# The opening of a hybrid layer: forget-gate columns behind the value weights, and their column chunk multiplied last

## The chip, the core and the metric

The kernel runs on one core of one Trainium2 chip. The metric is the device time of one execution in microseconds. The core has a matrix engine (TensorE, PE in the profile), three engines that work on tiles in SBUF and PSUM (VectorE = DVE, ScalarE = ACT, GpSimd = POOL), and SyncE (SP), which only issues transfers. Each engine runs its own instructions in order and waits on semaphores.

## What is computed

One inference step of a layer with two parallel branches, for 1024 prompt rows and 64 sample rows of width 1024. What matters here is its beginning:

```python
xn = rms_norm(x, g_pre)
z = xn @ w_in
sizes = (W_A, W_A, W_B, W_B, W_B, W_B, N_HEADS_B, D_MODEL, D_MODEL)
xa, ga, q, k, v, gb, fl, ma, mb = jnp.split(z, np.cumsum(sizes)[:-1], axis=-1)
...
logf = jax.nn.log_sigmoid((fl + b_f).astype(jnp.float32))
```

`w_in` is 1024 x 8208. The value columns `v` (1024 of them) and the forget-gate columns `fl` (16, one per head) are the two pieces that the opening computes. The rest (a recurrence in branch A, attention in branch B, the merge, the output projection, a gated embedding) follows in the same program and is not touched.

## The kernel before

All large products are made from halves: a float32 operand is split into a high part (rounded to the matrix engine's 32-bit format) and a low part (the remainder), and a product is three matmuls, high x high, high x low and low x high. ACT makes the high part (a copy), DVE the low part (a subtraction).

The opening multiplies the normalised rows of x, 128 at a time ("blocks" 0 to 8), with 1040 columns: 1024 value columns and the 16 forget-gate columns behind them. These lie in `wvh` and `wvl` (high and low), as eight slices along the contraction, k = 0 to 7, of 128 rows each. The columns are cut into three chunks, `VCH`: two of 352, and a third of 336 that holds the last 320 value columns and the 16 of the forget gate. The third chunk thus needs the value weights of a slice and the forget-gate columns.

For blocks 0 and 1 the work is written by slices, so that it can begin as soon as the first weights are there (lines 461 to 553). `load_wv(k)` (line 333) transfers 128 x 1024 value weights of slice k; slices 3 and 4 go to buffers of their own, the others share three buffers named `wv_raw`, so that slices 5, 6 and 7 can be loaded only when slices 0, 1 and 2 have been split. `wv_hi(k)` and `wv_lo(k)` (lines 341 and 344) split them. `x_hi` and `x_lo` (lines 417 and 421) scale and split the transposed x of one block and slice, which lies in PSUM. `rows(b, ks, cs, ps)` (line 451) issues the matmuls of block b for slices ks and chunks cs, in the order high x high, low x high, high x low of x and the weights. The PSUM tiles of the first two chunks are named `vacc`, that of the third `acc`. The latter are taken from the pool `mm` with two buffers, which block 1's transposed x (`tp`) holds until its last slice has been split.

The forget-gate columns come in one transfer of 16 floats for each of 1024 rows (`wf_raw`, line 434), written between the loads of slices 4 and 5, and are split for all slices at once (lines 493 and 494), between slices 3 and 4.

Two rules set the order. The order of PE, and in lines 461 to 545 that of ACT and DVE, is as written. SP's order is chosen by a scheduler when the program is built, from what is ready. Each transfer of SP or ACT also takes one of eight semaphores in turn and waits until the transfer that had it before has landed.

Behind the opening `evac_v` (line 524) copies finished chunks out of PSUM and stores them, `norm_x` and `turn_x` prepare the next blocks, and blocks 2 to 8 are multiplied chunk by chunk (from line 596, matmuls on lines 166 to 168).

Of the kernel before, what the change touches and what calls it, by code (L numbers as in the profile page):

```python
# [7 lines left out]
F32 = mybir.dt.float32  # L8
# [5 lines left out]
P = 128  # L14
D = 1024
KT = D // P
# [51 lines left out]
def hybrid_step(tc, a, o):  # L68
    nc = tc.nc
    PSUM = bass.MemoryType.PSUM  # L70
    act, dve, pool, pe, sp = nc.scalar, nc.vector, nc.gpsimd, nc.tensor, nc.sync
# [5 lines left out]
    def ps(name, bufs=1):  # L77
        return Pool(tc, name=name, bufs=bufs, space=PSUM, reuse_waits="tile")

    def f(ap):  # L80
        return ap.bitcast(F32)

    def copy_act(out, in_, scale=1.0):
        return act.activation(out=out, in_=in_, func=AF.Copy, scale=scale)  # L84

    def sub(eng, out, in0, in1):
        return eng.tensor_tensor(out=out, in0=in0, in1=in1, op=ALU.subtract)  # L87
# [194 lines left out]
    def panel(eng=None):  # L282

        look_ahead()
        if not ahead:
            return None
        split_next(eng or dve)
        tag, _, w, *_ = ahead.popleft()
        look_ahead()
        split_next(eng or dve)  # L290
        look_ahead()
        return tag, w
# [7 lines left out]
    mm = ps("mm", bufs=2)  # L300
# [14 lines left out]
    wvh = p1.tile([P, KT, 1040], F32R, name="wvh")  # L315
    wvl = p1.tile([P, KT, 1040], F32R, name="wvl")
    wf_raw = p1.tile([P, KT, NH], F32, name="wf_raw")
# [7 lines left out]
    def load_x(b):  # L325
        src, n, _ = x_src[b]
        t = p1x.tile([P, D], F32, name="x_in", tag="x_in", bufs=2)
        sp.dma_start(t[:n, :], src)
        x_in.append(t)
# [3 lines left out]
    def load_wv(k):  # L333
        if k in (3, 4):
            raw = raw_half[k - 3]
        else:
            raw = p1x.tile([P, D], F32, name="wv_raw", tag="wv_raw", bufs=3)
        sp.dma_start(raw[:, :], w_in[k * P:(k + 1) * P, C_V:C_V + D])
        raws[k] = raw

    def wv_hi(k):
        copy_act(wvh[:, k, :D], raws[k][:, :])

    def wv_lo(k):
        sub(dve, wvl[:, k, :D], raws.pop(k)[:, :], f(wvh[:, k, :D]))
# [23 lines left out]
    def norm_x(b):  # L369
        square_x(b)  # L370
        rstd_x(b)
        scale_x(b)

    def turn_x(b):
        _, n, t0 = x_src[b]
        xn = x_nm.pop(b)
        for g in range(2):
            tp = p1t.tile([P, 4, P], F32, name="tp", tag="tp")
            for j in range(4):
                k = 4 * g + j  # L380
                pe.transpose(tp[:, j, :n], xn[:n, k * P:(k + 1) * P], ident[:n, :n])
            h, l = XH[g][:, :, t0:t0 + n], XL[g][:, :, t0:t0 + n]
            copy_act(h, tp[:, :, :n])
            sub(dve, l, tp[:, :, :n], f(h))
            if n == DEC:
                pool.tensor_copy(xsl[:, 4 * g:4 * g + 4, :DEC], f(h))
                pool.tensor_copy(xsl[:, 4 * g:4 * g + 4, DEC:], f(l))
# [29 lines left out]
    def x_hi(b, ks):  # L417
        for k in ks:
            copy_act(xs[k][0][:, b * P:(b + 1) * P], turned[b][k // 4][:, k % 4, :], scale=gT[:, k:k + 1])

    def x_lo(b, ks):
        for k in ks:
            h, l = (t[:, b * P:(b + 1) * P] for t in xs[k])
            dve.scalar_tensor_tensor(out=l, in0=turned[b][k // 4][:, k % 4, :], scalar=gT[:, k:k + 1], in1=f(h),
                                     op0=ALU.mult, op1=ALU.subtract)
# [3 lines left out]
    load_x(0)  # L429
    act.dma_start(g8[:, :], a["g_pre"].rearrange("(k p) -> k p", p=P))  # L430
    load_x(1)
    for k in range(5):
        load_wv(k)
    sp.dma_start(wf_raw[:, :, :], w_in[:, C_FL:C_FL + NH].rearrange("(k p) n -> p k n", p=P))
    for k in range(5, KT):
        load_wv(k)
    wake = p1t.tile([P, 512], F32, name="wake", tag="tp")
    g_p = mm.tile([P, 512], F32, name="g_p", tag="acc")
    for i in range(WAKE):
# [4 lines left out]
    def weights(k, c):  # L444
        c0, w = VCH[c]
        return wvh[:, k, c0:c0 + w], wvl[:, k, c0:c0 + w]


    pair = [[p1v.tile([P, 512], F32, name="vacc", tag="vacc") for _ in range(2)] for b in range(2)]

    def rows(b, ks, cs=range(3), ps=(0, 2, 1)):
        for k in ks:
            xh, xl = (t[:, b * P:(b + 1) * P] for t in xs[k])
            for p in ps:
                for c in cs:
                    w = VCH[c][1]
                    wh, wl = weights(k, c)
                    pe.matmul(pair[b][c][:, :w], xl if p == 2 else xh, wl if p == 1 else wh,
                              start=(k == 0 and p == 0), stop=(k == KT - 1 and p == 1))
# [8 lines left out]
    def halves_of(b, ks):  # L468
        x_hi(b, ks)
        x_lo(b, ks)  # L470
# [12 lines left out]
    rows(0, [1], (0, 1))  # L483
    halves_of(1, (0, 1))
    rows(1, (0, 1), (0, 1))
    for k in (2, 3):
        halves_of(0, [k])
        wv_hi(k)
        wv_lo(k)
        halves_of(1, [k])  # L490
        rows(0, [k], (0, 1))
        rows(1, [k], (0, 1))
    copy_act(wvh[:, :, D:], wf_raw[:, :, :])
    sub(dve, wvl[:, :, D:], wf_raw[:, :, :], f(wvh[:, :, D:]))
    pair[0].append(mm.tile([P, 512], F32, name="acc", tag="acc"))
    rows(0, range(4), [2])
    for k in (4, 5):
        halves_of(0, [k])
        wv_hi(k)
        wv_lo(k)  # L500
        halves_of(1, [k])
        rows(0, [k])
        rows(1, [k], (0, 1))
    for k in (6, 7):
        halves_of(0, [k])
        halves_of(1, [k])
    pair[1].append(mm.tile([P, 512], F32, name="acc", tag="acc"))
    rows(1, range(6), [2])
    sp.dma_start(g_pre[:, :], a["g_pre"].partition_broadcast(P))
    load_x(2)  # L510
    load_x(3)
# [12 lines left out]
    def evac_v(b, c, acc):  # L524
        _, n, t0 = x_src[b]
        v_out = o["v_prompt"][t0:t0 + n, :] if b < NBLK else o["v_sample"]
        c0, w = VCH[c]
        wv = min(w, D - c0)
        v_sb = p1.tile([P, VCH[0][1]], F32, name="v_sb", tag="v_sb", bufs=3)
        copy_act(v_sb[:n, :wv], acc[:n, :wv])  # L530
        if b == NBLK:
            lo = p1.tile([DEC, VCH[0][1]], F32, name="v_lo", tag="v_lo", bufs=1)
            copy_act(lo[:, :w], acc[DEC:, :w])
            dve.tensor_tensor(out=v_sb[:n, :wv], in0=acc[:n, :wv], in1=lo[:, :wv], op=ALU.add)
        act.dma_start(v_out[:, c0:c0 + wv], v_sb[:n, :wv])
        if wv < w:
            dve.tensor_tensor(out=fl[:n, b, :], in0=acc[:n, wv:w], in1=bf[:n, :], op=ALU.add)
            if b == NBLK:
                dve.tensor_tensor(out=fl[:n, b, :], in0=fl[:n, b, :], in1=lo[:, wv:w], op=ALU.add)

    for k in (6, 7):
        wv_hi(k)
        wv_lo(k)
    norm_x(2)
    opening.__exit__(None, None, None)
    rows(0, (6, 7))
    for c in range(3):
        evac_v(0, c, pair[0][c])
    rows(1, [6])
    turn_x(2)  # L550
    rows(1, [7])
    for c in range(3):
        evac_v(1, c, pair[1][c])

# [41 lines left out]
    for b in range(2, NBLK + 1):  # L596
        _, n, t0 = x_src[b]
        for c, (_, w) in enumerate(VCH):
            acc = p1v.tile([P, 512], F32, name="vacc", tag="vacc")
# [382 lines left out]
    rows = p2.tile([P, LS], F32, name="prs", tag="prs", bufs=1)[:6, :]  # L982
# [459 lines left out]
    mm = ps("mm8", bufs=8)  # L1442
# [547 lines left out]
    for of in range(KT):  # L1990
# [15 lines left out]
        elif of == 1:  # L2006
            left_over = []
            finish_held(of, lambda *args: left_over.append(args))
            tag, w = panel()
            for args in left_over:  # L2010
                evac_a(*args)
        else:
            if of > 2:
                tag, w = panel()
# [224 lines left out]
    mm = ps("mm9", bufs=8)  # L2239
# [217 lines left out]
    b = B7[-1]  # L2457
# [71 lines left out]
```

## Time and profile before

| | |
|---|---|
| time of the runs, median of 3 | 1425.78 us (1425.51 to 1425.80) |
| span of the profiled execution | 1425.7 us |
| PE busy | 1401.0 us, 98% |
| DVE, ACT, POOL busy | 901.7, 728.6, 379.7 us |
| first matmul of block 2 (line 166) | 37.01 us |

In the rows of a timeline stand start, length, engine, line, operation, what is written from what, the shape and the count; in brackets how long the engine stood idle before and what released it. In the rows of windows stand the stretch, its length, PE's busy time and instructions, the mean granted clock of PE (1.00 is full), the share of the DMA engines' time and GB/s. Matmuls are pipelined and their ends modelled, so that two in a row overlap in these times.

### The profile page before, as it was taken

Reading aid. Unit: us, or ns where it says so; the run is one execution under the profiler, and the core shown is the slowest. Engines: PE = TensorE matmul, PEld = TensorE weight load, DVE = VectorE, ACT = ScalarE, POOL = GpSimd, SP = SyncE. Lnnn points to the kernel's source line nnn. Section 1 sums busy time; section 2 is a strip of 40 time slices with the busy share of each in tenths; the row PEclk is TensorE's granted clock in tenths of the full one; section 3 lists DMA queues with packets and bytes.
Section 4 is the critical chain, followed back from the end, with each engine's and each line's share of the span. In section 5 each row is a group of like instructions: output and inputs, shape, how many; then the busy total and the mean of one; then the engine's idle time right before and its main releaser. Section 6 shows DMA issues by size and latency. Waiting matters only on the chain.

```text
span 1425.7 us, 24345 instructions
## 1 busy us (share of the span) xinstructions
PE 1401.0 (98%) x9063; PEld 1331.9 (93%) x9063; DVE 901.7 (63%) x1563; ACT 728.6 (51%) x1338; POOL 379.7 (27%) x485
## 2 busy tenths in 40 slices
PE   9999999999999999999999899999999999999996
PEld 8999999999999999999999889999999998888885
DVE  6546665665653466667676567798845866338644
ACT  5414444444332566666666558778624434324533
POOL 0002332423321355455544430010001564000000
PEclk9999999999999999999999999999999999999999
DMA  5376655655336858757567434242283667224111
GB/s 204 123 131 109 114 168 178 189 158 171 95 76 183 217 150 148 177 125 178 131 155 163 65 89 57 44 61 48 79 299 126 213 215 281 91 76 146 49 49 44
DMA packets 141074, 191.64 MB, mean 134 GB/s; under 512 B 24580, under 2 KB 99372, under 8 KB 140956
## 3 DMA queue, kind: packets, MB, share of 16 engines
q1 hardware_dynamic: 119308, 149.43, 42.7%
q10 hardware_dynamic: 17104, 27.32, 5.3%
q0 software_dynamic: 4544, 13.34, 3.3%
q8 instruction: 71, 1.16, 0.4%
q14 instruction: 47, 0.39, 0.1%
HBM read 127.11 MB, written 62.92 MB: 133 GB/s over the span
## 4 chain that ended last, share of the span: by engine, by line
PE 89%; DMA 5%; DVE 2%; ACT 1%; issue 1%; SPq 1%; POOL 0%; DVEq 0%; ACTq 0%; POOLq 0%
PE quad L811 19%; PE acc L166 13%; PE acc L167 12%; PE acc L168 12%; PE quad_b L2129 5%; PE tp L1196 4%; PE pv L1240 2%; PE pv L1238 2%; PE s L1171 2%; PE s L1170 2%; DMA d_ma<-st 1%; PE vacc L166 1%; DMA w_raw<-in_w_in 1%; PE vacc L167 1%; PE vacc L168 1%; DMA d_y<-y 1%
## 5 line engine op out<-in xcount | busy, mean ns | idle before, releaser
L166 PE MATMUL acc<-xh,wh 128*128 128x368 f32 (+1 forms) x672 | 228.0, 339 | 0.4
L167 PE MATMUL acc<-xl,wh 128*128 128x368 f32 (+1 forms) x672 | 220.1, 328 | 0.0
L168 PE MATMUL acc<-xh,wl 128*128 128x368 f32 (+1 forms) x672 | 219.7, 327 | 0.0
L166 PEld LDWEIGHTS acc<-xh,wh 128*128 128x128 f32 x672 | 126.8, 189 | 1.9 <-DVE nm L1150 1.3
L167 PEld LDWEIGHTS acc<-xl,wh 128*128 128x128 f32 x672 | 127.0, 189 | 0.6
L168 PEld LDWEIGHTS acc<-xh,wl 128*128 128x128 f32 x672 | 126.7, 189 | 0.0
L84 ACT ACTIVATE th<-tp 128x512 fp32r<-128x512 f32 (+1 forms) x160 | 86.6, 549 | 65.9 <-PE tp L1196 61.5
L87 DVE TENSOR_TENSOR tl<-tp,th 128x512 fp32r<-128x512 f32 (+1 forms) x160 | 99.2, 634 | 30.4 <-ACT th L84 29.1
L87 DVE TENSOR_TENSOR wl<-w_raw,wh 128x1024 fp32r<-128x1024 f32 (+1 forms) x67 | 76.8, 1148 | 59.6 <-ACT wh L84 40.8
L84 ACT ACTIVATE wh<-w_raw 128x1024 fp32r<-128x1024 f32 (+1 forms) x67 | 62.7, 938 | 91.2 <-PE quad L811 37.5
L811 PE MATMUL quad<-xh,wh 128*128 128x272 f32 x448 | 93.9, 291 | 0.0
L811 PE MATMUL quad<-xl,wh 128*128 128x272 f32 x448 | 92.6, 288 | 0.0
L811 PE MATMUL quad<-xh,wl 128*128 128x272 f32 x448 | 92.5, 288 | 0.0
L1156 POOL TENSOR_SCALAR pb<-pb,sm 128x640 f32<-128x640 f32 (+1 forms) x64 | 61.4, 960 | 95.1 <-DVE sm L1155 87.3
L1238 PE MATMUL pv<-tl,vv 128*128 128x512 f32 x192 | 70.8, 369 | 6.1 <-DVE y L1254 5.4
L1153 ACT ACTIVATE pb<-pb,nm 128x640 f32<-128x640 f32 (+1 forms) x64 | 63.3, 989 | 25.9 <-DVE nm L1150 23.2
L84 ACT ACTIVATE wh<-s 128x512 fp32r<-128x512 f32 x54 | 34.0, 631 | 74.6 <-PE quad L811 48.3
L811 PEld LDWEIGHTS quad<-xl,wh 128*128 128x128 f32 x448 | 70.6, 188 | 0.0
L811 PEld LDWEIGHTS quad<-xh,wh 128*128 128x128 f32 x448 | 70.2, 188 | 0.2
L811 PEld LDWEIGHTS quad<-xh,wl 128*128 128x128 f32 x448 | 70.4, 188 | 0.0
L1150 DVE CUSTOM_DVE_ANT_0 pb<-s,mask 128x640 f32<-128x640 f32 (+1 forms) x64 | 65.0, 1015 | 4.4 <-PE s L1171 4.2
L1170 PE MATMUL s<-k,q 128*128 128x128 f32 (+2 forms) x192 | 67.4, 358 | 0.0
(692 smaller groups left out, 3958.5 us busy)
## 6 DMA issues: line engine op xcount, KB each, us to landing
w_raw<-in_w_in SPq DMA_DIRECT2D x56, 256.0 KB
q<-d_q SPq DMA_DIRECT2D x48, 256.0 KB
k<-d_k SPq DMA_DIRECT2D x48, 256.0 KB
w_raw<-in_w_in SPq DMA_DIRECT2D x56, 128.0 KB
wraw<-in_w_in SPq DMA_DIRECT2D x24, 256.0 KB
w_raw<-in_w_branch SPq DMA_DIRECT2D x24, 256.0 KB
d_k<-oh ACTq DMA_DIRECT2D x16, 272.0 KB
d_k<-kl SPq DMA_DIRECT2D x16, 272.0 KB
```

The costliest lines, as they stand in the source:

```text
L84: return act.activation(out=out, in_=in_, func=AF.Copy, scale=scale)
L87: return eng.tensor_tensor(out=out, in0=in0, in1=in1, op=ALU.subtract)
L166: pe.matmul(out, ah, bh, start=start, stop=False)
L167: pe.matmul(out, ah, bl, start=False, stop=False)
L168: pe.matmul(out, al, bh, start=False, stop=stop)
L811: pe.matmul(acc[:, c, :CW], l[:, k, :], r[:, k, c * CW:(c + 1) * CW], start=(first and k == 0 and p == 0), stop=(k == 3 and p == 2), skip_ ...
L1150: at = book("D", now[0] + HOP_PE, per(D_MAX, n), lambda: dve.tensor_tensor_reduce(out=pr[:, :n], in0=s[:, :n], in1=m, scale=-1.0, scalar=- ...
L1153: at = book("A", at, per(A_EXP, n), lambda: act.activation(out=pr[:, :n], in_=pr[:, :n], func=AF.Exp, scale=-1.0, bias=nm, accum_out=sm))
L1156: return free, book("G", at, per(G_NORM, n), lambda: pool.tensor_scalar(out=pr[:, :n], in0=pr[:, :n], scalar1=sm, scalar2=1.0, op0=ALU.mul ...
L1170: pe.matmul(s[:, c0:c0 + w], t["q1"][:, q], t["k1"][:, c0:c0 + w], start=True, stop=False)
L1238: pe.matmul(pv[:, 512 - n:], v, tl[:, c:c + n], start=(j == 0), stop=False)
L2129: pe.matmul(acc[:, c, :CW], l[:, k, :], r[k // 2][:, k % 2, c * CW:(c + 1) * CW], start=(first and k == 0 and p == 0), stop=(k == 3 and p ...
```

## The change

The load of the forget-gate columns is written behind all eight loads of value weights. Slices 2 to 7 are handled by one loop, first and second chunk for both blocks. Then follow the split of the forget-gate columns, the two `acc` tiles, and the third chunk for all eight slices of block 0 and then block 1, with the transposes of block 2 before block 1's last two slices.

```diff
     load_x(1)
-    for k in range(5):
+    for k in range(KT):
         load_wv(k)
     sp.dma_start(wf_raw[:, :, :], w_in[:, C_FL:C_FL + NH].rearrange("(k p) n -> p k n", p=P))
-    for k in range(5, KT):
-        load_wv(k)
...
-    for k in (2, 3):
+    for k in range(2, KT):
         halves_of(0, [k])
         wv_hi(k)
         wv_lo(k)
         halves_of(1, [k])
         rows(0, [k], (0, 1))
         rows(1, [k], (0, 1))
-    copy_act(wvh[:, :, D:], wf_raw[:, :, :])
-    sub(dve, wvl[:, :, D:], wf_raw[:, :, :], f(wvh[:, :, D:]))
-    pair[0].append(mm.tile([P, 512], F32, name="acc", tag="acc"))
-    rows(0, range(4), [2])
-    for k in (4, 5):
-        halves_of(0, [k])
-        wv_hi(k)
-        wv_lo(k)
-        halves_of(1, [k])
-        rows(0, [k])
-        rows(1, [k], (0, 1))
-    for k in (6, 7):
-        halves_of(0, [k])
-        halves_of(1, [k])
-    pair[1].append(mm.tile([P, 512], F32, name="acc", tag="acc"))
-    rows(1, range(6), [2])
...
-    for k in (6, 7):
-        wv_hi(k)
-        wv_lo(k)
+    copy_act(wvh[:, :, D:], wf_raw[:, :, :])
+    sub(dve, wvl[:, :, D:], wf_raw[:, :, :], f(wvh[:, :, D:]))
     norm_x(2)
     opening.__exit__(None, None, None)
-    rows(0, (6, 7))
+    for b in range(2):
+        pair[b].append(mm.tile([P, 512], F32, name="acc", tag="acc"))
+    rows(0, range(KT), [2])
     for c in range(3):
         evac_v(0, c, pair[0][c])
-    rows(1, [6])
+    rows(1, range(6), [2])
     turn_x(2)
-    rows(1, [7])
+    rows(1, (6, 7), [2])
```

What this makes of the program is seen best in the order of the instructions. First PE before, from the last slice of the third chunk that was multiplied early (nine rows like the first three stand ahead) through slice 4 of block 0 and block 1. The names ending in 113 and 115 are the high and low x of slices 0 to 3, those in 114 and 116 of slices 4 to 7.

```order
L458 MATMUL acc<-wvh,xh_113 128x336
L458 MATMUL acc<-wvh,xl_115 128x336
L458 MATMUL acc<-wvl,xh_113 128x336
L458 MATMUL vacc<-wvh,xh_114 128x352 x2
L458 MATMUL acc<-wvh,xh_114 128x336
L458 MATMUL vacc<-wvh,xl_116 128x352 x2
L458 MATMUL acc<-wvh,xl_116 128x336
L458 MATMUL vacc<-wvl,xh_114 128x352 x2
L458 MATMUL acc<-wvl,xh_114 128x336
L458 MATMUL vacc<-wvh,xh_114 128x352 x2
L458 MATMUL vacc<-wvh,xl_116 128x352 x2
L458 MATMUL vacc<-wvl,xh_114 128x352 x2
```

The same place on PE in the changed program: slice 3 of block 1, then slice 4 of block 0 and of block 1.

```order
L456 MATMUL vacc<-wvh,xh_113 128x352 x2
L456 MATMUL vacc<-wvh,xl_115 128x352 x2
L456 MATMUL vacc<-wvl,xh_113 128x352 x2
L456 MATMUL vacc<-wvh,xh_114 128x352 x2
L456 MATMUL vacc<-wvh,xl_116 128x352 x2
L456 MATMUL vacc<-wvl,xh_114 128x352 x2
L456 MATMUL vacc<-wvh,xh_114 128x352 x2
L456 MATMUL vacc<-wvh,xl_116 128x352 x2
L456 MATMUL vacc<-wvl,xh_114 128x352 x2
```

Fifteen matmuls of the third chunk (twelve of slices 0 to 3, three of slice 4) have left the place between slice 3 and slice 5; all 48 of that chunk now stand behind slice 7.

ACT in the changed program, from the split of slice 3 to the split of the forget-gate columns:

```order
L84 ACTIVATE wvh<-w_raw 128x1024
L84 ACTIVATE xh_113<-tp,gT 128x128
L84 ACTIVATE xh_114<-tp,gT 128x128
L84 ACTIVATE wvh<-w_raw 128x1024
L84 ACTIVATE xh_114<-tp,gT 128x128 x2
L84 ACTIVATE wvh<-wv_raw 128x1024
L84 ACTIVATE xh_114<-tp,gT 128x128 x2
L84 ACTIVATE wvh<-wv_raw 128x1024
L84 ACTIVATE xh_114<-tp,gT 128x128 x2
L84 ACTIVATE wvh<-wv_raw 128x1024
L84 ACTIVATE xh_114<-tp,gT 128x128
L494 DMA bf<-in_b_f 128x16
```

The split of the forget-gate columns, which stood between the first two rows of x, is the next row behind these; the splits of slices 6 and 7 no longer stand behind all five remaining pieces of x. DVE follows the same order.

Third, SP in the changed program, from the loads of slices 0 to 2 on:

```order
L338 DMA wv_raw<-in_w_in 128x1024 x3
L338 DMA w_raw<-in_w_in 128x1024 x2
L434 DMA wf_raw<-in_w_in 128x8x16
L491 DMA g_pre<-in_g_pre 128x1024
L495 DMA lp<-in_cache_logf 128x16
L501 DMA vec<-in_conv_w 32x128
L501 DMA vec<-in_conv_b 8x128
L328 DMA x_in<-in_x_prompt 128x1024
L338 DMA wv_raw<-in_w_in 128x1024 x2
L328 DMA x_in<-in_x_prompt 128x1024
L338 DMA wv_raw<-in_w_in 128x1024
```

Before, the same transfers stand in the same order, here and to the end of SP's program: nothing has moved. The scheduler issued the forget-gate columns ahead of slices 5 to 7 in both programs, since these wait for a buffer and the columns do not.

## The prediction

> **What bounds the kernel now.** I read the page's head first, for who is busy, then the chain of waits, cut to the opening that the change touches.
>
> ```profile
> span 1425.7 us, 24345 instructions
> PE 1401.0 (98%) x9063; PEld 1331.9 (93%) x9063; DVE 901.7 (63%) x1563; ACT 728.6 (51%) x1338; POOL 379.7 (27%) x485
> ```
>
> TensorE (PE) is busy for 98% of the span, so a microsecond that it idles in the opening is a microsecond at the end, unless a later wait takes it back. The span, 1425.7 us, is also what the runs show (median 1425.78), so a sum against one holds for the other. What a measurement of this kernel can tell from no change is about 0.2%, 2.85 us.
>
> The chain of waits between 10 and 40 us (start, length, what) shows what the opening waits for:
>
> ```profile
> 13.93 9.37 DMA wv_raw<-in_w_in
> 23.32 1.07 ACT wvh L84
> 24.41 1.23 DVE wvl L87
> 27.12 0.36 DVE xl L424
> 27.53 3.05 PE acc L458 x18
> ```
>
> The bound is a transfer: the value weights of k = 5, issued at 13.93 and landed at 23.32, then their split on ACT and DVE. Why 9.4 us? The timeline of SP's queue, and what SP itself waited for, tell when transfers landed:
>
> ```profile
> 5.14 0.65 SPq L434 DMA_DIRECT2D wf_raw<-in_w_in  x1
> 13.46 0.36 SPq L328 DMA_DIRECT2D x_in<-in_x_prompt  x1
> 13.93 1.17 SPq L338 DMA_DIRECT2D wv_raw<-in_w_in  x2
> 18.70 0.33 SPq L328 DMA_DIRECT2D x_in<-in_x_prompt  x1
> 22.05 0.27 SPq L519 DMA_DIRECT2D vec<-in_state_h  x1
> 23.32 0.30 SPq L519 DMA_DIRECT2D vec<-in_state_conv  x1
> ...
> SPq L328 <- DMA wf_raw<-in_w_in: 3.5, 1, 3.5
> SPq L519 <- DMA wv_raw<-in_w_in: 1.0, 1, 1.0
> SPq L519 <- DMA x_in<-in_x_prompt: 0.6, 1, 0.6
> ```
>
> SP stood until 18.70 for the forget-gate columns, until 22.05 for a block of x, until 23.32 for k = 5. The windows of the same stretch (length, PE busy and count, clock, DMA share, GB/s) show the engines of the DMA nearly idle in between:
>
> ```profile
> 15.00:17.00 2.00, 2.00 (x14) 1.00 0.16 42
> 17.00:19.00 2.00, 2.00 (x15) 1.00 0.96 377
> 25.00:27.00 2.00, 1.96 (x13) 1.00 0.11 41
> ```
>
> So the forget-gate columns (16 floats per row) hold up what stands behind them, and after 25 us only a remainder flows. PE does not feel most of this, because before k = 5 arrives it has the third column chunk to multiply. Its timeline, with ACT's two relevant rows:
>
> ```profile
> 15.07 0.37 ACT L84 ACTIVATE xh<-tp,gT 128x128 fp32r<-128x128 f32 x1
> 18.66 0.31 ACT L84 ACTIVATE wvh<-wf_raw 128x128 fp32r<-128x128 f32 x1 [3.22 <-DMA wf_raw<-in_w_in]
> 19.42 0.32 PE L458 MATMUL acc<-wvh,xh 128*128 128x336 f32 x1
> 21.27 0.49 PE L458 MATMUL vacc<-wvh,xh 128*128 128x352 f32 x2
> 23.34 0.48 PE L458 MATMUL vacc<-wvl,xh 128*128 128x352 f32 x2
> 24.44 0.59 PE L458 MATMUL vacc<-wvh,xh 128*128 128x352 f32 x2 [0.62 <-ACT wvh L84]
> 25.34 0.31 PE L458 MATMUL acc<-wvh,xl 128*128 128x336 f32 x1
> 25.70 0.59 PE L458 MATMUL vacc<-wvl,xh 128*128 128x352 f32 x2
> 26.93 0.48 PE L458 MATMUL vacc<-wvl,xh 128*128 128x352 f32 x2
> 27.53 0.42 PE L458 MATMUL acc<-wvh,xh 128*128 128x336 f32 x1
> 30.42 0.49 PE L458 MATMUL vacc<-wvh,xh 128*128 128x352 f32 x2
> ```
>
> One matmul shows 0.32 and a pair 0.48, so in a stream each starts 0.16 after the one before; twelve 336-column ones fill 19.42 to 21.27, 0.154 each. Durations overlap, so I count from start to start. Lost now, between 19.42 and 30.42: 24.44 against 23.66 (23.34 + 0.32), 0.78; 25.70 against 25.50 (25.34 + 0.16), 0.20; 27.53 against 27.25 (26.93 + 0.32), 0.28; and each first matmul behind a gap takes 0.1 more (0.59 against 0.49, 0.42 against 0.32), 0.30. Together 1.56. The check: 24 x 0.16 + 36 x 0.154 = 9.4 of work in 11.0.
>
> **The load.** The source puts the forget-gate load last, but SP's program is unchanged: it still comes ahead of the loads of k = 5 to 7, which wait for their buffers. Nothing that releases SP moves before 20 us either (the splits of k = 0 to 2, the landings). So I take this edit at nothing: the columns land at 18.7 and k = 5 at 23.32 as now.
>
> **ACT and DVE.** ACT no longer stands 3.22 us for the columns, so k = 4 is split from about 15.4 on instead of 19.13. PE wants it at 19.42; nothing is gained there, since PE had work until then.
>
> **The order of the multiplications.** The work is the same; what moves is the cover. From 19.42 PE has only the twelve 352-column matmuls of k = 4: 12 x 0.16 = 1.92, until 21.34. The fifteen of the third chunk that bridged the rest are gone behind k = 7. The first matmul of k = 5 still comes at 24.44, so 3.10 are lost plus 0.10 for the start. Then hi and lo pairs of block 0 run until 25.18; the next pair needs the low half of the weights, ready for 25.70: 0.52 plus 0.10. Block 1 of k = 5 ends at 27.09 (25.70 + 0.1 + 8 x 0.16). For k = 6: x at 22.05 and k = 5 at 23.32 landed 1.27 apart, so I estimate 24.6 for k = 6, and two landings later 27.1 for k = 7 (after 27 us the queues are all but empty, 0.02 in the next row). Splits at 1.07 on ACT and 1.23 on DVE make k = 6 ready by 27.4, wanted at 27.09 (high half, ready 26.0) and 27.73 (low half); k = 7 high by 28.2, wanted at 29.01, low by 29.5, wanted at 29.65. No loss, with 0.2 to spare at the last. The wait at 27.53, for a PSUM bank that block 1's transposed x still held, disappears: the bank is wanted only from 30.9. From there 48 matmuls of the third chunk take 7.4, as they do now in pieces.
>
> ```profile
> 27.00:28.00 1.00, 0.88 (x6) 1.00 0.02 2
> ...
> 30.00:37.00 7.00, 7.00 (x48) 1.00 0.36 96
> ```
>
> Lost then: 3.20 + 0.62 = 3.82, against 1.56: **+2.26 us**. Bounds: had k = 7 slipped half a microsecond, +2.7; had k = 5 landed half a microsecond earlier (the landings of a block lie 1.27 apart, less than half of that is plausible), +1.8. What comes behind is covered: block 2's x is transposed behind the same 6 matmuls or more, its first block 1 evacuations stand ahead of it on ACT but some 2 us early, and PE idles nowhere between 30 and 37 us now (7.00 of 7.00).
>
> **The clock, where the delay meets it later.** The windows show the granted clock at half twice, after long gaps. PE's long wait and the windows around it, cut on a grid of 3.41 us:
>
> ```profile
> 809.00 0.79 PE L1238 MATMUL pv<-tl,vv 128*128 128x512 f32 x1 [4.05 <-DVE y L1254]
> ...
> 804.26:807.68 3.42, 0.69 (x5) 1.00 0.67 186
> 807.68:811.09 3.41, 2.09 (x7) 0.50 0.00 0
> 811.09:814.50 3.41, 3.41 (x14) 0.50 0.00 0
> 814.50:817.92 3.42, 3.42 (x22) 1.00 0.18 61
> 831.57:834.98 3.41, 2.14 (x14) 1.00 0.00 0
> ...
> 1415.26:1418.67 3.41, 0.00 (x0) 1.00 0.00 0
> 1418.67:1422.08 3.41, 0.00 (x0) 0.50 0.40 154
> ```
>
> The changes fall at 807.68, 814.50 and 1418.67; the last is 179 steps of 3.413 behind the first. A stretch with 0.69 of 3.41 busy (20%) brought half clock, one with 2.14 (63%) did not, and at half clock one with 2.09 (61%) did not bring full clock back. PE worked from 809.0 to 814.50 at half speed, 2.75 lost. Four executions lie within 0.3 us of each other, so I think the grid is tied to the start. Then work that comes 2.26 later meets it otherwise: the gap lies at 807.2 to 811.3, the stretch to 811.09 is empty, the next one is full, and only 811.3 to 814.5 is slow: 1.62 instead of 2.75, **-1.1**. If the grid is not tied, or a wait behind eats it, 0. I take -0.8, nearer the full value, because of the four executions.
>
> Sum: 1425.8 + 2.26 - 0.8 = **1427.2 us**.
>
> **Rivals.** First, slower: the new gap is itself long enough to bring the clock down. By the rows above the stretch 22.61 to 26.02 would hold 24.44 to 25.42 and 25.70 to 26.02, 1.30 of 3.41, 38%. That lies between 20% (came down) and 63% (did not); it decides from wherever in between the limit is. Price: half speed from 26.02 to 29.44, 1.71. The total shift of 3.97 then puts the later gap at 808.9 to 813.0, where the stretches hold 36% and 45%; full clock returns at 817.9, 2.47 lost instead of 2.75. Sum 2.26 + 1.71 - 0.28 = +3.7, 1429.5. For it: the gap of 2.94 without any matmul is longer than the 2.73 between PE's last end (804.95) and the drop at 807.68. Against it: 38% is nearly twice 20%.
>
> [...]
>
> Second: the later gap gives nothing back (the grid runs freely, or POOL, whose spans are rough, holds the work behind 833 us): 1425.8 + 2.26 = 1428.0.
>
> Third: the load does move, or the columns hold up less. If k = 5 landed 3.1 earlier, at 20.2, PE would lose nothing in the opening: 1425.8 - 1.56 = 1424.2. For it speaks the nearly idle stretch 15 to 17; against it that SP's program is the same instruction by instruction.
>
> **How the numbers follow.** Clock stays up in the opening: 56 in 100, of which 40 with the later slow stretch shortened and 16 without it (second rival). First rival 37, third 4, rest 3. The forecast's own range is 1426.4 to 1428.5. For 8 in 10 it must reach over the first rival: 1426.2 to 1429.9. Slower by over 0.2% (beyond 1428.6): the first rival, less the part in which the later gap brings no drop at all, and a little of the second: 0.36. Faster by over 0.2% (below 1422.9) needs more than the whole opening holds: 0.03. Within: 0.61.
>
> **What would show it.** SP's queue as now, with k = 5 landing near 23.3. One wait of PE of about 2.9 us until 24.4 for the high half of k = 5, a second near 25.2 to 25.7 for the low half, none at 27.5; the third chunk from about 30.9, block 2 from about 39.3 instead of 37.0. The granted clock at 26.02 tells the first rival, the slow stretch behind 811 us the second. Wrong would be: k = 5 landing by 21, a wait for k = 7, or a wait in block 2's transposes.

## The result, and the profile after

The changed kernel takes **1429.05 us** (median of 9, 1427.94 to 1430.17) against 1425.53 us (median of 9) for the kernel before on the same chip: ratio 1.0024, 95% interval 1.0016 to 1.0032. It is slower by 3.5 us (2.3 to 4.6). The forecast was 1427.2 in a range of 1426.2 to 1429.9; the result lies in the range, but nearer the first rival (1429.5) than the forecast. It lies above the forecast's own range (1426.4 to 1428.5) and is slower by more than 0.2%, for which 36 in 100 were given; what took it in is that the wide range was drawn over the first rival. One execution of the kernel before (7919.69 us) and one of the pure delay below (2313.54 us) were far longer than all others of their kernels and are in no ratio.

First the opening of the changed kernel. SP's timeline and ACT's rows of the value weights (start, length, what; later line numbers are 2 to 18 lower than before):

```profile
4.24 0.45 SPq L434 DMA_DIRECT2D wf_raw<-in_w_in  x1
13.87 0.93 SPq L338 DMA_DIRECT2D wv_raw<-in_w_in  x2
18.01 0.33 SPq L328 DMA_DIRECT2D x_in<-in_x_prompt  x1
23.24 0.30 SPq L501 DMA_DIRECT2D vec<-in_state_conv  x1
...
23.25 1.06 ACT L84 ACTIVATE wvh<-wv_raw 128x1024 fp32r<-128x1024 f32 x1 [5.84 <-DMA wv_raw<-in_w_in]
27.04 1.06 ACT L84 ACTIVATE wvh<-wv_raw 128x1024 fp32r<-128x1024 f32 x1 [0.56 <-DMA wv_raw<-in_w_in]
```

The load of the forget-gate columns is still issued among the first transfers, and the weights of k = 5 land at 23.24, as before. PE's timeline of the same stretch:

```profile
21.08 0.49 PE L456 MATMUL vacc<-wvl,xh 128*128 128x352 f32 x2
24.36 0.59 PE L456 MATMUL vacc<-wvh,xh 128*128 128x352 f32 x2 [2.79 <-ACT wvh L84]
25.61 0.58 PE L456 MATMUL vacc<-wvl,xh 128*128 128x352 f32 x2 [0.34 <-DVE wvl L87]
30.83 0.32 PE L456 MATMUL acc<-wvh,xh 128*128 128x336 f32 x1
39.11 0.32 PE L166 MATMUL vacc<-wvh,xh 128*128 128x352 f32 x1
```

PE waits 2.79 us where it waited 0.62, and block 2 begins at 39.11 instead of 37.01: 2.10 later. The third chunk stands behind the first two. In the chain of waits the same transfer carries the opening, and behind it PE runs through:

```profile
13.87 9.36 DMA wv_raw<-in_w_in
23.25 1.06 ACT wvh L84
24.34 1.24 DVE wvl L87
25.61 5.38 PE vacc L456 x32
30.99 6.48 PE acc L456 x42
```

The span of this execution is 1426.8, only 1.1 more than the span that the profile before showed, while the medians lie 3.5 apart. A run's time is its span and about 1.7 more (1428.49 for this one, and 1.6 to 1.8 in the other profiled executions whose time is known), so the profiled execution of before took 1427.4, an estimate, and was one of its late ones. What made it late matters below.

### The profile page after: what moved, and what is told of

Same layout as the page of the kernel before. It is cut to its first block, busy times and chain, and to the rows that moved or that the text cites. A ratio compares the mean times of both kernels' runs of the same rounds, so it can differ in the third digit from the quotient of the medians.

```text
span 1426.8 us, 24341 instructions
## 1 busy us (share of the span) xinstructions
PE 1400.1 (98%) x9063; PEld 1331.7 (93%) x9063; DVE 902.0 (63%) x1563; ACT 727.7 (51%) x1338; POOL 376.3 (26%) x485
## 4 chain that ended last, share of the span: by engine, by line
PE 89%; DMA 5%; DVE 2%; ACT 1%; SPq 1%; issue 1%; POOL 0%; DVEq 0%; ACTq 0%; POOLq 0%
PE quad L794 19%; PE acc L166 13%; PE acc L167 12%; PE acc L168 12%; PE quad_b L2112 5%; PE tp L1179 4%; PE pv L1223 2%; PE pv L1221 2%; PE s L1154 2%; PE s L1153 2%; DMA d_ma<-st 1%; PE vacc L166 1%; DMA w_raw<-in_w_in 1%; PE vacc L167 1%; PE vacc L168 1%; DMA d_y<-y 1%
## 5 line engine op out<-in xcount | busy, mean ns | idle before, releaser
L1136 ACT ACTIVATE pb<-pb,nm 128x640 f32<-128x640 f32 (+1 forms) x64 | 63.3, 989 | 26.0 <-DVE nm L1133 23.2
```

What stands on the lines that cost most here:

```text
L1136: at = book("A", at, per(A_EXP, n), lambda: act.activation(out=pr[:, :n], in_=pr[:, :n], func=AF.Exp, scale=-1.0, bias=nm, accum_out=sm))
```

## The experiments

Where a difference of two experiments is given, it is of medians; an interval is that of a ratio to the kernel before on the same chip. Rows of windows here show the busy time and count not only of PE but of five engines, in this order: PE, PE's weight loads (PEld), DVE, ACT, POOL; then the clock, the share of the DMA engines' time and GB/s.

### The changed kernel again

> The changed kernel itself, once more, for its profile and its clock. In its first comparison it was 3.5 us slower (1429.05 against 1425.53), while its profiled execution shows block 2 begin 2.1 us later (39.11 against 37.01) and full clock in the opening. Theory C (lost cover alone): +2.1 us, and the rest is spread between executions. Theory K (the clock also falls in the opening's new gap, in some executions): +3 to +4, and in a profile where it falls the granted clock is 0.50 for 3.4 us somewhere between 22 and 30 us.

Measured: 1430.03 us, ratio 1.0022 (1.0013 to 1.0032). The eleven times do not lie around one value: five are from 1427.2 to 1428.6, five from 1430.0 to 1430.6, and one is 1432.87. (The nine times of the result, 1427.94 to 1430.17, do not part into groups in this way.) The profile caught the longest, 1432.87 (span 1431.2). PE's timeline in its opening:

```profile
24.25 0.58 PE L456 MATMUL vacc<-wvh,xh 128*128 128x352 f32 x2 [2.62 <-ACT wvh L84]
25.51 0.95 PE L456 MATMUL vacc<-wvl,xh 128*128 128x352 f32 x2 [0.36 <-DVE wvl L87]
...
40.47 0.32 PE L166 MATMUL vacc<-wvh,xh 128*128 128x352 f32 x1
```

A pair that took 0.58 takes 0.95 from 25.51 on. The windows show why; their edges are set at the moments when the granted clock changed:

```profile
21.85:25.26 3.41, 0.90 (x4) 0.61 (x4) 1.03 (x1) 2.12 (x4) 0.00 (x0) 1.00 0.68 263
25.26:28.67 3.41, 3.16 (x11) 3.16 (x12) 3.01 (x7) 2.76 (x7) 0.00 (x0) 0.50 0.03 9
28.67:32.08 3.41, 3.41 (x23) 3.41 (x22) 2.59 (x15) 2.98 (x8) 0.00 (x0) 1.00 0.02 4
```

The clock was at half from 25.26 to 28.67, behind a stretch that was 26% busy (0.90 of 3.41). Block 2 began 1.36 later than in the profile above. Here are the same windows of that profile. In each of the eight profiles that show more than one change of the clock, the changes lie whole steps of 3.4133 us apart to within 0.1 us (the figure is worked out below); in this one those at 811.65, 815.07 and 1419.22 lie 1 and 177 steps apart. No change lies in its opening, so the edges are set on this grid to within 0.03 us, counted back from 811.65 and 815.07, an estimate:

```profile
19.78:23.19 3.41, 1.79 (x12) 1.49 (x10) 0.00 (x0) 0.00 (x0) 0.00 (x0) 1.00 0.99 394
23.19:26.60 3.41, 1.90 (x10) 1.61 (x11) 2.27 (x4) 3.14 (x6) 0.00 (x0) 1.00 0.28 108
26.60:30.01 3.41, 3.41 (x23) 3.41 (x22) 2.89 (x7) 2.97 (x6) 0.00 (x0) 1.00 0.03 5
```

The gap is the same (2.79 against 2.62 us), but here the estimated edge at 23.19 falls into it, both stretches are over half busy (1.79 and 1.90 of 3.41), and the clock stayed at 1.00. So the first rival's drop is real, and what differs between these two executions is where the grid lies: edges at 25.26 and, a step ahead of it, 21.85 in one, at 19.78, 23.19 and 26.60 in the other.

### The gap filled with idle products

An idle product is a matmul whose result nothing reads.

```diff
     for k in range(2, KT):
...
+        if k == 5:
+            pair[0].append(mm.tile([P, 512], F32, name="acc", tag="acc"))
+            for _ in range(17):
+                pe.matmul(pair[0][2][:, :352], xs[0][0][:, :P], wvh[:, 0, :352], start=True, stop=True)
...
-    for b in range(2):
-        pair[b].append(mm.tile([P, 512], F32, name="acc", tag="acc"))
+    pair[1].append(mm.tile([P, 512], F32, name="acc", tag="acc"))
```

> The changed kernel with 17 idle matmuls (352 columns, into a PSUM tile that is overwritten later) between slices 4 and 5 of block 0, so that TensorE is busy for 2.7 us of the gap but waits for the same weights. Theory C: no faster than the changed kernel (+2.1 to +3.5 against the kernel before), since the wait is the cost. Theory K: the clock cannot fall in the opening any more, so about 1 us faster than the changed kernel, +2.1 against before.

Measured: 1425.61 us, ratio 1.0000 (0.9991 to 1.0009). PE does 17 products more, block 2 begins at 38.81, and yet all of the loss is gone. Neither theory had that: both expected at least 2.1 us over the kernel before.

### A delay without a gap

```diff
+    late = mm.tile([P, 512], F32, name="late", tag="acc")
+    for _ in range(13):
+        pe.matmul(late[:, :352], xs[0][0][:, :P], wvh[:, 0, :352], start=True, stop=True)
```

This stands in the kernel before, between blocks 1 and 2.

> The kernel before with 13 idle matmuls (352 columns, 2.1 us) between block 1 and block 2, so that everything behind 37 us comes 2.1 us later and nothing else changes. Theory C: +2.1 us, the delay goes through to the end. If a later wait takes it back: 0. If the shift alone costs clock at the long wait near 805 us: more than +2.1, up to +3.5; if it saves there as I had counted: +1.3.

Measured: 1425.28 us, ratio 0.9995 (0.9986 to 1.0004). A delay of 2.1 us costs nothing at the end. So lateness alone could be taken back somewhere, and the extra time of the change could not yet be put down to the lost cover.

### The load really moved

```diff
-        sp.dma_start(raw[:, :], w_in[k * P:(k + 1) * P, C_V:C_V + D])
+        tc.keep_in_program_order(sp.dma_start(raw[:, :], w_in[k * P:(k + 1) * P, C_V:C_V + D]))
...
-    sp.dma_start(wf_raw[:, :, :], ...)
+    tc.keep_in_program_order(sp.dma_start(wf_raw[:, :, :], ...))
```

> The changed kernel with SP's loads of the value weights and the forget-gate columns held in the written order, so that the columns are really sent behind slice 7. Theory C (the wait for slice 5 behind the columns is the cost): slice 5 lands by 16 us instead of 23.3, TensorE waits for nothing between 19 and 31 us, block 2 begins near 35.4 instead of 39.1, so -1.5 us against the kernel before. Rival: the columns are not what holds slice 5 up (SP's own waits do), slice 5 lands after 20 us and the time stays above the kernel before.

Measured: 1424.96 us, ratio 0.9996 (0.9987 to 1.0005). The queue and ACT's row of k = 5:

```profile
15.67 0.38 SPq L338 DMA_DIRECT2D wv_raw<-in_w_in  x1
16.10 0.42 SPq L434 DMA_DIRECT2D wf_raw<-in_w_in  x1
...
17.85 1.06 ACT L84 ACTIVATE wvh<-wv_raw 128x1024 fp32r<-128x1024 f32 x1 [0.56 <-DMA wv_raw<-in_w_in]
```

With the columns truly behind, k = 5 lands at 17.8 instead of 23.2 and block 2 begins at 35.32. That the forget-gate columns hold up what stands behind them is thereby shown (with them one load of 4 KB changed its place in the queue); yet the end gains nothing that can be told from no change. Expected were a landing by 16 us and 1.5 us less at the end, and neither came.

### Where the delay is taken back

In all seven profiles of the table below PE waits near 805 us for the copy of a product out of PSUM (DVE `y`), which waits for a transfer of the earlier `y` to land, and the clock falls to 0.50 there. Two rows of that chain for the kernel before, and two for the pure delay:

```profile
796.52 0.59 POOL d_y L1227
797.11 10.42 DMA d_y<-y
```

```profile
797.52 0.59 POOL d_y L1230
798.12 9.05 DMA d_y<-y
```

The transfer began 1.0 later and landed 0.4 earlier. The place by profile ("slow" is half of the time that PE worked there at half clock, from the clock's edges, an estimate: a pair of 128x352 products took 0.95 at half clock above, and takes 0.48 in a stream at full clock):

| kernel | block 2 | d_y from | took | PE waited | slow | span |
|---|---|---|---|---|---|---|
| before | 37.01 | 797.11 | 10.42 | 4.05 | 2.75 | 1425.7 |
| before again (last experiment) | 36.76 | 796.89 | 9.92 | 3.58 | 1.52 | 1423.4 |
| changed | 39.11 | 799.82 | 9.85 | 3.49 | 1.70 | 1426.8 |
| changed again | 40.47 | 802.42 | 10.38 | 4.04 | 3.15 | 1431.2 |
| gap filled | 38.81 | 798.74 | 8.92 | 2.58 | 1.70 | 1424.6 |
| pure delay | 38.26 | 798.12 | 9.05 | 2.70 | 1.70 | 1424.0 |
| load moved | 35.32 | 794.97 | 10.23 | 3.89 | 1.70 | 1422.5 |

Wait and slow stretch make 4.3 to 7.2 us there, and the two late kernels that lost nothing at the end have the smallest sums. Each row is one execution, and the two of the kernel before differ by 1.7 in this sum. To see what the opening costs by itself, this place had to go. The planner that orders PE in that stage does not know how long the transfer takes. Told it for the one copy that waits, it puts other work of the same stage in front of the waiting product:

```diff
-    y_of, gate_of = {}, {}
+    y_of, gate_of, y_lands = {}, {}, [0.0]
...
-        at = book_first("A", now[0] + HOP_PE, A_LO, lambda: copy_act(y, pv[other, :]))
-        at = book_first("D", at, D_Y, join)
+        at = max(now[0] + HOP_PE, y_lands[0] if u == 27 else 0.0)
+        at = book_first("D", book_first("A", at, A_LO, lambda: copy_act(y, pv[other, :])), D_Y, join)
...
-            nxt = []
+            nxt, y_lands[0] = [], at + 9500.0
```

> Edit: the kernel before, with the planner told when the 10-us transfer of y lands, so that other matrix work stands in PE's queue ahead of the one value product that waited about 4 us for it near 805 us; about 210 PE rows near 800 us change places, nothing else. In the profile of before, the wait there is 4.1 us and the half clock behind it costs 2.75 us; in the other profiles 2.6 to 4.0 and 1.7. If the place costs what these rows say, the wait and the slow stretch go: 1425.8 - 4.3 to 6.8 = 1419.0 to 1421.5. If the wait only moves to another place, 1425.8. It is also the base of the three runs beside it, in which nothing can be taken back at that wait.

Measured: **1419.78 us**, ratio 0.9957 (0.9944 to 0.9969), the fastest version here together with its repeat below. The windows of the place, the kernel before and then this one:

```profile
795.00:815.00 20.00, 15.95 (x89) 14.57 (x88) 10.98 (x28) 9.71 (x23) 8.76 (x14) 0.83 0.58 58
```

```profile
795.00:815.00 20.00, 20.00 (x130) 18.89 (x129) 13.82 (x37) 12.81 (x28) 9.51 (x16) 1.00 0.60 67
```

PE is busy throughout and the clock stays at 1.00. With the place gone, three openings were compared with this one, the base, on the same chip.

### The changed kernel, the pure delay and the moved load without that place

The edit of the planner, put into the changed kernel, the pure delay and the moved load.

> Edit: the changed kernel with the same rows moved near 800 us. Theory A (the new opening gap costs its lost cover, 2.1 us, and in about half of the executions a slow stretch of 3.41 us, 1.7 more; the later wait gave part of it back or added to it): 2.1 to 3.9 over the run before it (before with the wait filled), median near +3.0. Theory B (only the clock in the gap counts, the lateness itself costs nothing anywhere): +0.0 in some and +1.7 in other executions. Theory C (the extra came from the later wait): no difference.

Measured: 1422.71 us (ratio 0.9983, 0.9975 to 0.9992), **2.9 over** the run before it. Two groups stand apart now: six from 1421.1 to 1422.7, five from 1424.1 to 1425.0, with medians of 1422.1 and 1424.9. That is theory A.

> Edit: the kernel before with 13 idle products (2.1 us) between blocks 1 and 2, and the rows near 800 us moved. With the wait in place the 2.1 us cost nothing (1425.3 against 1425.8). If the wait near 805 us swallowed them (shorter wait, shorter slow stretch): 2.1 us over before with the wait filled. If another place swallows them: the same as that.

Measured: 1421.89 us (0.9971, 0.9959 to 0.9982), **2.1 over** the base, which is what was inserted; the times spread over some 1.7 us in each of the two. So it was the place near 805 us that had swallowed the delay.

> Edit: the changed kernel with the forget-gate columns really loaded behind all value weights, and the rows near 800 us moved. The opening of that kernel ended 1.7 us earlier than before's in its profile, yet its time was only 0.8 lower. If the later wait swallowed the rest: 1.5 to 2 us below before with the wait filled. If something else holds the end: the same as that.

Measured: 1420.35 us (0.9957, 0.9943 to 0.9971), not below the base of 1419.78: a miss. The base's own profile gives a reason. Its k = 5 landed early and its opening lost almost nothing:

```profile
21.70 1.06 ACT L84 ACTIVATE wvh<-wv_raw 128x1024 fp32r<-128x1024 f32 x1 [1.90 <-DMA wv_raw<-in_w_in]
35.54 0.32 PE L166 MATMUL vacc<-wvh,xh 128*128 128x352 f32 x1
```

With the load moved block 2 began at 35.35. By these profiles only 0.2 were left to gain, where I had reckoned with 1.7 from one profile of each. That is not the whole account: in the base's repeat below block 2 begins at 36.26, and the profile of the moved load waits 1.53 us near 471 us and then runs a stretch at half clock (last section), where the base's waits 0.63 and keeps the clock. Whether its other executions do the same was not seen.

### The two parts of the loss

The changed kernel with the wait filled and the 17 idle products in the opening gap:

> Edit: the changed kernel with 17 idle products (2.7 us) in the opening gap, and the rows near 800 us moved. Without the idle products that kernel's executions fell into two groups, 1421.1 to 1422.7 (six) and 1424.1 to 1425.0 (five). If the upper group is the clock that fell in the gap: one group, near 1422 (2.1 to 2.8 over before with the wait filled, the lost cover alone), none above 1423.5. If the groups come from the landing of the value weights alone: two groups again, median 1422.7.

Measured: 1420.98 us (0.9963, 0.9951 to 0.9975), all five times between 1420.4 and 1422.0. The upper group is gone: were it still 5 in 11, five times would all miss it about once in twenty. With the half clock that a profile shows in this gap (25.26 to 28.67, the changed kernel again), and the loss that went when the gap was filled above, I put the group down to the clock. This run is 1.2 over the base measured beside it (1419.82, below), and its forecast was 2.1 to 2.8; five times with an interval of 1.7 either way don't decide between 1.2 and 2.1.

Next, the cover, in the changed kernel with the wait filled: 12 of the 15 third-chunk products of block 0 and the split of their columns put back in front of slice 4, and so of k = 5.

```diff
     for k in range(2, KT):
+        if k == 4:
+            copy_act(wvh[:, :, D:], wf_raw[:, :, :])
+            sub(dve, wvl[:, :, D:], wf_raw[:, :, :], f(wvh[:, :, D:]))
+            pair[0].append(mm.tile([P, 512], F32, name="acc", tag="acc"))
+            rows(0, range(4), [2])
...
-    rows(0, range(KT), [2])
+    rows(0, range(4, KT), [2])
```

> Edit: the changed kernel with 12 of the 15 third-chunk products of block 0 put back in front of k = 5 (and the split of their columns before them), and the rows near 800 us moved. The cover theory: 1.9 of the lost 2.1 to 2.8 come back, no gap is long enough for the clock, so within 0.7 us of before with the wait filled (1419.8). If the order of what comes behind k = 7 (block 1's part of the third chunk, still last) is what costs: near 1422.

Measured: 1419.75 us (0.9952, 0.9940 to 0.9964), the median of the base beside it to within 0.1, where the times of either spread over 2 to 3 us; block 2 begins at 35.53, and from 10 us on no wait of PE over 0.2 us is left in the opening. With twelve products back ahead of k = 5 the loss is gone; the new order of the rest costs nothing that can be measured.

> Edit: the kernel before with the rows near 800 us moved, once more, as the base of the two runs beside it on the same chip: 1419 to 1421, one group.

Measured: 1419.82 us (0.9953, 0.9941 to 0.9965), one group, block 2 from 36.26 in its profile. Both versions with the wait filled and the cover in place thus beat the kernel before by some 6 us and the changed one by some 9.

### The kernel before, once more

> No edit: the kernel before, for a second profile of it. The profiled execution of before had a span of 1425.7, where a run's time is its span and 1.7 more, so it was a late one: 1427.4 against a median of 1425.8. If its lateness lay where the forecast's base was read, this profile shows k = 5 landing before 23.3, less than 1.5 us lost in the opening and block 2 from 35.5 to 36.5; the wait near 805 us 2.6 to 4.1 and the half clock behind it 1.7 to 2.8.

Measured: 1425.59 us, ratio 0.9994 (0.9985 to 1.0002), span of the profiled execution 1423.4. Expected was a landing before 23.3 (it is 23.08), under 1.5 lost in the opening and block 2 between 35.5 and 36.5 (it is 36.76, a miss by 0.3); near 805 us a wait of 2.6 to 4.1 (it is 3.58) and 1.7 to 2.8 lost at half clock (it is 1.52, a miss by 0.2). Its later place, in PE's timeline and then in windows on its grid:

```profile
808.28 0.79 PE L1238 MATMUL pv<-tl,vv 128*128 128x512 f32 x1 [3.58 <-DVE y L1254]
```

```profile
804.48:807.89 3.41, 0.23 (x2) 0.00 (x0) 0.36 (x1) 0.95 (x2) 0.00 (x0) 1.00 0.43 145
807.89:811.31 3.42, 3.03 (x11) 2.73 (x12) 3.39 (x14) 2.48 (x9) 0.78 (x2) 0.50 0.00 0
811.31:814.72 3.41, 3.41 (x24) 3.32 (x23) 1.89 (x5) 2.28 (x5) 1.29 (x2) 1.00 0.04 10
```

Here one stretch is slow, not two: 1.52 lost instead of the 2.75 on which the forecast was built, and 0.47 less wait. These 1.7 are most of the 2.3 by which the two spans of the same kernel differ.

## Why the prediction was right and wrong

**The load: right.** "I take this edit at nothing." SP's queue is as before, k = 5 landed at 23.24 against a forecast 23.3. The moved load shows that the third rival's mechanism exists (k = 5 at 17.8); it isn't what this change does.

**The cover: right, in place and size.** Forecast were a wait of 2.94 until 24.44, measured 2.79 until 24.36; a second until 25.70, measured 25.61; none at 27.5, and there is none; k = 7 at 27.1, measured 27.04; the third chunk from 30.9, measured 30.83; block 2 at 39.3, measured 39.11. Over all profiles in which the clock stayed up in the opening and nothing was inserted there, block 2 begins at 35.54 to 37.01 in the old order (four) and at 38.34 and 39.11 in the new (two): 36.4 against 38.7 on average, +2.3 for the +2.26 of the sum. Twelve products back ahead of k = 5 take the loss away. The size rests on few profiles; by the times, the lower group with the wait filled lies 2.4 over its base, and the run with the gap filled as well 1.2. The "lost now" of 1.56 came from an execution at the late end: in the others with the old order PE lost less in the opening, and in that of the base almost nothing. "A sum against one holds for the other" does not hold: time and span are 1.7 apart, and the two numbers met only because the profiled execution was late.

**The later gap's -0.8: wrong.** This is the step of the forecast that failed. It rested on "I think the grid is tied to the start". The clock's changes do lie on a grid within each of the eight profiles that show more than one: in the changed kernel's second profile the change at 813.74 stands 231 steps behind the one at 25.26 and the change at 1424.73 stands 410 steps behind it, of 3.4133 us each (1399.47 / 410). But the phase, the remainder of a change's time after whole steps, is 2.13 in the profile of before, 2.34 in its second, 2.69 and 1.37 in those of the changed kernel, and over all fourteen profiles it lies anywhere from 0.28 to 2.69 (in six of them it is read from one change alone). So in these runs the grid is not tied to the start; what sets it is not shown. The slow stretch of 2.75 belonged to that execution and not to the kernel; the other one in the old order lost 1.5 there. So there was nothing that a later start could be sure to get back. The changed kernel lost 1.70 and 3.15. The 1.70 is near the 1.62 that was forecast, but by luck: it came at another phase than the one from which the 1.62 was worked out. I had decided for the tied grid because four executions lay within 0.3 us of each other. The record has three such times; the profile's span of 1425.7 lies beside them only as a span, and the nine times of the result spread from 1423.59 to 1427.41.

**The first rival: right in kind, and not a matter of all or nothing.** I gave 37 in 100 that the clock falls in the new gap. It falls in some executions of the same kernel and not in others: by the groups in 6 of 11 with the wait in place and in 5 of 11 with it filled, an estimate, since one profile alone shows the drop. Its price was forecast as 1.71. Between the two profiles of the changed kernel block 2 moves by 1.36; the groups' medians lie 2.7 apart, which is more. Those two profiles show where more can come from: by the transfer near 800 us (table above) they are 2.60 apart, and on the way PE waits longer at the same products, 0.81 against 0.38 and 1.42 against 0.70. First the profile with the clock up, then the other:

```profile
102.20 0.43 PE L166 MATMUL vacc<-wvh,xh 128*128 128x352 f32 x1 [0.38 <-DVE fl L519]
491.25 0.30 PE L1154 MATMUL s<-k,q 68*128 68x128 f32 x1 [0.70 <-DMA k<-d_k]
```

```profile
103.97 0.43 PE L166 MATMUL vacc<-wvh,xh 128*128 128x352 f32 x1 [0.81 <-DVE fl L519]
493.49 0.30 PE L1154 MATMUL s<-k,q 68*128 68x128 f32 x1 [1.42 <-DMA k<-d_k]
```

That these waits grow whenever the clock falls in the gap is not shown. The sum in place of the forecast's, without the -0.8 and with half of a price of 1.4 to 2.7: 1425.8 + 2.3 + 0.7 to 1.4 = 1428.8 to 1429.5, against 1429.05 measured; it is made afterwards, from these runs.

**The second rival** (nothing given back, 1428.0) has the right sum for the lower group, 1427.2 to 1428.6 in the run of the changed kernel again.

**Open.** Why the place near 805 us swallows the 2.1 of the pure delay and nothing of the changed kernel's. The length of the transfer goes with it (8.92 and 9.05 against 9.85 and 10.38, one profile of each), but it doesn't go with its start, and what else sets it wasn't tried. How much the place took back is as uncertain: its wait and slow stretch are 4.40 in the pure delay, 2.4 less than in the first profile of the kernel before and 0.7 less than in the second.

## What to carry to other kernels

Work that stands in front of a late transfer can pay twice: here it covered the wait (0.62 us of PE's time in place of 2.79) and kept the clock at 1.00 where a profile without it shows 0.50, and a dozen products of 0.15 us were worth 2.9 us. When a term of the forecast is read from where the clock's grid lies, it is, in this kernel's profiles, a property of that execution (the phase runs from 0.28 to 2.69 of 3.41 us): take the average over its phases, and profile the kernel twice before building on a stall that one profile shows. What a delay far ahead of a wait for a transfer does to the end can be hidden until that wait is taken out of both kernels: here 2.1 us cost nothing with the wait in place (1425.28) and 2.1 without it (1421.89 against 1419.78).

## What was not expected of the hardware

In these profiles the busy share of a stretch, as the profile counts it, doesn't sort by itself what the clock does next. Stretches with 1.79 and 1.90 of 3.41 busy in the opening kept full clock; in the moved load with the wait filled one with 1.88 lost it, near 470 us:

```profile
469.75:473.16 3.41, 1.88 (x13) 1.63 (x12) 1.52 (x3) 2.11 (x4) 0.40 (x1) 1.00 0.90 272
473.16:476.58 3.42, 3.42 (x14) 3.35 (x13) 1.57 (x7) 1.62 (x7) 3.17 (x6) 0.50 0.23 57
```

On the way back, a half-clock stretch with 3.03 of 3.42 busy (89%, the second profile of before) returned to full clock, and one with 2.87 (84%, the changed kernel again) was followed by another slow one:

```profile
813.74:817.15 3.41, 2.87 (x11) 2.58 (x12) 3.38 (x13) 2.53 (x8) 0.67 (x2) 0.50 0.00 0
817.15:820.57 3.42, 3.42 (x14) 3.42 (x14) 1.88 (x7) 1.89 (x4) 1.39 (x3) 0.50 0.01 2
```

And the same opening's transfers land up to 1.6 us apart between executions: k = 5 between 21.70 and 23.32 in the six profiles with the opening of before.
